# RG-LRU gate products one column tile later, the exponentials pinned behind the sigmoids, the delta rule's output split before the lz tiles, the rotary key's low part on GpSimd

## The chip, the cores and the metric

The kernel runs on one core of a Trainium2 chip. Its time is the device time of one execution in microseconds; where several runs are told, their median counts. The engines are named as the profile names them: PE (TensorE, matrix products; PEld is its loading of weights), DVE (VectorE), ACT (ScalarE), POOL (GpSimd) and SP (SyncE, which issues the DMA transfers).

## The reference

Two layers of an autoregressive trunk over 1024 tokens with 1024 features. Each layer normalises its input, projects it once to a wide row, hands slices of that row to three mixers, multiplies each mixer's output by a gate `silu(...)` from the same projection, and projects the 2048 gathered columns back, added to the input:

```
h = rmsnorm(x) ; proj = h @ w_in           # slices: q k v b a gz | mq mkv mkr mz | lx lz
A) o_a = rmsnorm(gated_delta_rule(...)) * silu(gz)             # 4 heads x 128
B) o_b = latent attention, 8 heads; the rotary key k_pe = rope(mkr) is shared by all heads; * silu(mz)
C) u = conv4(lx) + bias                                        # RG-LRU, 512 channels, 8 blocks of 64
   r = sigmoid(u @ w_r + b_r) ; i = sigmoid(u @ w_i + b_i)     # block-diagonal
   a = exp(-8 r softplus(-L)) ; b = sqrt(-expm1(2 log a)) * (i * u)
   h_t = a_t h_(t-1) + b_t ; o_c = h * silu(lz)
x = x + concat(o_a, o_b, o_c) @ w_out
```

The change touches mixer C, the way in which o_a comes to the output projection, and the rotary key of mixer B.

## The kernel before

**Layout and products.** Features lie on the 128 partitions, the 1024 tokens along the free axis; a half is 512 tokens (`H2`). Every operand of a product is kept as two tiles of type fp32r, a high and a low part (x = hi + lo). `mm3` issues three matmuls for each pair: ah·bh, ah·bl, al·bh (lines 121 to 123). `split` makes the two parts of an activation: a copy on ACT (line 127) and a subtraction on DVE or POOL (line 128). `load_w` does it for weights: a DMA into `wst`, the cast `whi` (on DVE for wide tiles, line 111; on ACT for narrow ones, line 109) and the subtraction `wlo` on POOL (line 112). `in_tile` makes one column tile of the input projection, 128 columns by 1024 tokens: 48 matmuls, 24 for each half, into a PSUM tile `pbig` of which there are two.

**The stage around the change.** After the delta rule of a layer, `lru` makes the four lx column tiles. For each column m it runs `conv` (one ACT step and three DVE steps, with raised priority), splits the result `u` by halves into `uh` and `ul` (the low part of the first half on POOL, of the second on DVE; one buffer each), loads the block-diagonal gate weights `w_lru[l, m]`, and makes the gate products: four groups of three matmuls into PSUM banks `pssc`, each followed by a sigmoid on ACT into `r` (tag lr) or `i` (tag li). Then u is multiplied by i, and tanh(8 r softplus) is taken into the tile of i (`th`). A second loop takes exp into the tile of r (now `a`), its square `a2` (tag lt, two buffers), and on DVE th = (a2 + 1) th, which is 1 - a² by way of the tanh. A third loop takes the square root, multiplies u by it and runs the scan (line 569). A fourth loop makes the four lz column tiles, the gate z (`silu2`: a tanh on ACT, a product on DVE; the tile z takes the slot of `uh` or `ul` in turn) and by halves `gate_split`: the product `of` on DVE (tag of, two buffers) and its split into `oh` and `ol` (POOL for columns 0 to 2, DVE for column 3). In `lru`'s text the delta rule's output comes last: four loads `oaf` from DRAM (tag li), each split into `oah` on ACT and `oal` on POOL.

**The output projection of this stage** (`out_proj`, called with `lru`'s result) goes over eight weight tiles of `w_o1`. Each has 48 matmuls, which read the four (oah, oal) pairs and the four (oh, ol) pairs by halves, into banks `pspr`; DVE adds a bank to the residual `xt` (line 92). There are three `xt` and two banks.

**The stage behind it** begins, still beside the output projection, with `split_latents`: five latents are loaded from DRAM and split, and the rotary key is turned (`rope`), copied twice into `kp` on ACT, and its low part `kl` is the difference, on DVE (line 663).

**What sets the order.** Each engine runs its instructions in an order that is fixed when the program is built. A scheduler picks them by priority: the place in the program's text, raised or lowered by `prio(±LOW)`, and by what is ready in its own model. `keep_in_program_order` pins one instruction behind the one traced before it on the same engine. So the text's order and the engines' order differ, and buffers (a tag with its number of slots) make a step wait until the reader of the slot's former content is done.

Of the kernel before, what the change touches and what calls it, by code (L numbers as in the profile page):

```python
# [9 lines left out]
F32 = mybir.dt.float32  # L10
F32R = mybir.dt.float32r
AF = mybir.ActivationFunctionType
ALU = mybir.AluOpType
AX = mybir.AxisListType

T = 1024
# [47 lines left out]
class Trunk:  # L64
# [18 lines left out]
        return self.ps.tile([128, H2], F32, name="ps" + tag, tag=tag)  # L83

    def act(self, out, in_, func, **kw):
        self.nc.scalar.activation(out, in_, func, **kw)  # L86

    def stt(self, out, in0, s, in1, op0, op1):
        self.nc.vector.scalar_tensor_tensor(out, in0, s, in1, op0, op1)  # L89
# [23 lines left out]
        return (hi[:, :n].rearrange("p (k c) -> p k c", k=nk),  # L113
                lo[:, :n].rearrange("p (k c) -> p k c", k=nk))

    def mm3(self, out, pairs):

        nc = self.nc
        n = len(pairs)
        for j, (ah, al, bh, bl) in enumerate(pairs):  # L120
            nc.tensor.matmul(out, ah, bh, start=(j == 0), stop=False)  # L121
            nc.tensor.matmul(out, ah, bl, start=False, stop=False)  # L122
            nc.tensor.matmul(out, al, bh, start=False, stop=(j == n - 1))  # L123

# [4 lines left out]


    def in_tile(self, l, *ms):

        if ms[0] not in self.ready:
            tiles = []
            for m in ms:
                hi, lo = self.early.pop(m, None) or self.load_w(self.i["w_in"][l, m], 8, 128)
                self.ready[m] = self.big()
                tiles.append((hi, lo, self.ready[m]))
            with self.prio(self.LOW):
                for n in range(2):  # L140
                    s = slice(n * H2, (n + 1) * H2)
                    for hi, lo, p in tiles:
                        self.mm3(p[:, s], [(hi[:, k], lo[:, k], self.hh[k][:, s], self.hl[k][:, s]) for k in range(8)])
        return self.ready.pop(ms[0])

    def conv(self, y, p, w, bias=None):

# [381 lines left out]
    def lru(self, l):  # L529
        nc, pa, par = self.nc, self.pa, self.par  # L530
        st, res = [], []
        for m in range(4):
            p = self.in_tile(l, MT_LX + m)
            u = pa.tile([128, T], F32, name="u", tag="lu", bufs=4)
            with self.prio(-self.LOW):
                self.conv(u, p, par[:, C_LCONV + 4 * m : C_LCONV + 4 * m + 4], bias=par[:, C_LCB + m : C_LCB + m + 1])
            uh = pa.tile([128, T], F32R, name="uh", tag="uh", bufs=1)
            ul = pa.tile([128, T], F32R, name="ul", tag="ul", bufs=1)
            for n, eng in ((0, nc.gpsimd), (1, nc.vector)):
                s = slice(n * H2, (n + 1) * H2)  # L540
                self.split(uh[:, s], ul[:, s], u[:, s], eng)
            hi, lo = self.load_w(self.i["w_lru"][l, m], 2, 128, pool=pa)
            gt = []
            for k in range(2):
                t = pa.tile([128, T], F32, name="lg", tag=("lr", "li")[k], bufs=4)
                cb = (C_LBR, C_LBI)[k] + m
                for n in range(2):
                    s = slice(n * H2, (n + 1) * H2)
                    pg = self.bank("sc")
                    self.mm3(pg, [(hi[:, k], lo[:, k], uh[:, s], ul[:, s])])  # L550
                    self.act(t[:, s], pg, AF.Sigmoid, bias=par[:, cb : cb + 1])
                gt.append(t)
            r, ii = gt
            self.tt(u, u, ii, ALU.mult)

            th = ii
            self.act(th, r, AF.Tanh, scale=self.c8[:, m : m + 1])
            st.append((u, r, th))
        for m in range(4):
            u, a, th = st[m]  # L560
            self.act(a, a, AF.Exp, scale=self.c8n[:, m : m + 1])
            a2 = pa.tile([128, T], F32, name="a2", tag="lt", bufs=2)
            self.act(a2, a, AF.Square)
            self.stt(th, a2, 1.0, th, ALU.add, ALU.mult)
        for m in range(4):
            u, a, th = st[m]
            self.act(th, th, AF.Sqrt)
            self.tt(u, u, th, ALU.mult)
            nc.vector.tensor_tensor_scan(th, a, u, 0.0, ALU.mult, ALU.add)
        for m in range(4):  # L570
            p = self.in_tile(l, MT_LZ + m)
            z = pa.tile([128, T], F32, name="lz", tag=("uh", "ul")[m % 2], bufs=1)
# [11 lines left out]
            res.append((oh, ol))  # L584
        for h in range(8 - self.MZ2, 8):
            self.gate_tile(l, MT_MZ + h, self.mzd[h], pa.tile([128, T], F32, name="z", tag="lt", bufs=2))
        oa = []
        for h in range(4):
            f = pa.tile([128, T], F32, name="oaf", tag="li", bufs=4)
            nc.sync.dma_start(f, self.oad[h])  # L590
            oh = pa.tile([128, T], F32R, name="oah", tag="lu", bufs=4)
            ol = pa.tile([128, T], F32R, name="oal", tag="lr", bufs=4)
            self.split(oh, ol, f, nc.gpsimd)
            oa.append((oh, ol))
        return oa + res


# [41 lines left out]
    def split_latents(self):  # L639
# [18 lines left out]
        for n in range(2):  # L658
            s = slice(n * H2, (n + 1) * H2)
            kr = self.rope(kx[0:64, s], 64, s)  # L660
            nc.scalar.copy(kp[0:64, s], kr)
            nc.scalar.copy(kp[64:128, s], kr)
            self.tt(kl[0:64, s], kr, kp[0:64, s].bitcast(F32), ALU.subtract)

            nc.scalar.copy(kl[64:128, s], kl[0:64, s].bitcast(F32))
        self.kp, self.kl = kp, kl
# [523 lines left out]
```

## Time and profile before

| | |
|---|---|
| Median of three runs | 2171.55 us (2168.96 to 2174.38) |
| The profiled execution, its own time | 2169.95 us |
| Its span | 2168.2 us |
| Mean granted clock of PE | 0.985 |
| ACT table loads | x81, 103.9 us |
| Low parts of weights on POOL (wlo) | x196, 316.2 us |

The span runs from the first to the last instruction of the profiled execution. Busy time counts the instructions that work on data; waiting in a queue is not in it. In rows of the timeline the first two numbers are the start (us from the span's start) and the duration, then engine, line, operation, output<-inputs and shape; a bracket at the end gives the idle time before the instruction on its engine and what ended it. Rows of grouped instructions have busy time and mean ns of one behind the first bar, and the idle time before them with its releaser behind the second. Rows of waits give engine, tile and line, what ended the wait, and then the idle time in us, the number of waits and the longest one. Rows of stretches give the stretch, its length, and the busy time of each engine with its number of instructions, the granted clock, the DMA share and GB/s. A row with x2 is two instructions that follow each other, drawn together.

### The profile page before, as it was taken

To read this page: it belongs to the slowest core of one execution; us is meant where nothing else is said; L and a number is where in the kernel's file an instruction comes from. 1 tells how busy PE (TensorE), PEld (TensorE's weight loads), DVE (VectorE), ACT (ScalarE), POOL (GpSimd) and SP (SyncE) were. 2 spreads that over 40 slices of the span, in tenths; PEclk is the share of its full clock that TensorE was granted. 3 is DMA by queue.
4 is the path that set the end of the run, shared out by engine and by line. 5 is a ranking of instruction groups with operands and counts; after the bars stand their busy time and mean duration, and the time that the engine had idled before them with its cause. 6 is when DMAs were issued, how large, how long until landed. Compare 5 with 4: busy or idle time off the path is not lost. (4 is left out here: it accounts for less than half of the span.)

```text
span 2168.2 us, 28796 instructions
## 1 busy us (share of the span) xinstructions
PE 2060.0 (95%) x10380; PEld 1685.0 (78%) x10380; DVE 1324.2 (61%) x2498; ACT 882.9 (41%) x1790; POOL 731.4 (34%) x784
## 2 busy tenths in 40 slices
PE   7999999999989999999899999999998999999997
PEld 4888877787768788878668888787876877878874
DVE  6647546555851777776675475474468337676766
ACT  6241344135720554444542413521376125444534
POOL 3222333234451333332241313333336323332322
PEclk9999999999999999999999999999999999999998
DMA  4223212323253116335421331134222520335172
GB/s 142 86 79 103 67 59 93 98 78 102 68 172 124 39 38 190 98 128 168 157 83 48 102 93 45 63 107 132 64 73 90 192 101 24 108 118 168 60 237 97
DMA packets 135103, 222.08 MB, mean 102 GB/s; under 512 B 37808, under 2 KB 60336, under 8 KB 134960
## 3 DMA queue, kind: packets, MB, share of 16 engines
q1 hardware_dynamic: 134960, 220.24, 31.3%
q8 instruction: 82, 1.34, 0.3%
q14 instruction: 61, 0.50, 0.1%
HBM read 147.31 MB, written 72.88 MB: 102 GB/s over the span
## 5 line engine op out<-in xcount | busy, mean ns | idle before, releaser
L112 POOL TENSOR_TENSOR wlo<-wst,whi 128x1024 fp32r<-128x1024 f32 (+3 forms) x196 | 316.2, 1614 | 831.0 <-DVE whi L111 302.0
L121 PE MATMUL pbig<-h,whi 128*128 128x512 f32 x1216 | 485.4, 400 | 9.2 <-ACT h L127 6.2
L123 PE MATMUL pbig<-h,wlo 128*128 128x512 f32 x1216 | 485.2, 399 | 4.0 <-POOL wlo L112 4.0
L122 PE MATMUL pbig<-h,whi 128*128 128x512 f32 x1216 | 484.5, 398 | 2.1 <-DVE h L128 1.0
L121 PEld LDWEIGHTS pbig<-h,whi 128*128 128x128 f32 x1216 | 231.4, 190 | 55.5 <-ACT h L127 7.0
L122 PEld LDWEIGHTS pbig<-h,whi 128*128 128x128 f32 x1216 | 230.7, 190 | 49.7 <-DVE h L128 3.5
L123 PEld LDWEIGHTS pbig<-h,wlo 128*128 128x128 f32 x1216 | 231.1, 190 | 48.8 <-POOL wlo L112 5.3
L86 ACT ACTIVATE P<-pS,mx,scq 128x512 f32<-128x512 f32 (+1 forms) x192 | 128.2, 671 | 154.0 <-DVE mx L89 82.5
L111 DVE CAST whi<-wst 128x1024 fp32r<-128x1024 f32 x92 | 78.5, 853 | 141.0 <-PE pbig L122 106.9
L95 POOL TENSOR_SCALAR P<-P,mx 128x128 f32<-128x128 f32 (+6 forms) x112 | 81.1, 725 | 211.3 <-DVE mx L778 128.6
L109 ACT CAST whi<-wst 128x256 fp32r<-128x256 f32 (+2 forms) x104 | 46.4, 446 | 203.8 <-DMA wst<-in_w_uk 100.0
L127 ACT CAST pth<-pstp 128x512 fp32r<-128x512 f32 x192 | 91.2, 479 | 75.4 <-PE pstp L807 75.4
L767 DVE TENSOR_REDUCE mx<-pS 128x1 f32<-128x512 f32 (+1 forms) x192 | 106.5, 555 | 16.6 <-PE pS L761 10.1
L128 DVE TENSOR_TENSOR ptl<-pstp,pth 128x512 fp32r<-128x512 f32 x192 | 104.8, 552 | 14.9 <-ACT pth L127 14.0
L86 ACT ACT_TABLE_LOAD x81 | 103.9, 1283 | 14.0 <-DVE kT L89 11.9
L807 PE MATMUL pstp<-con,P 128*128 128x128 f32 x576 | 98.1, 275 | 5.7 <-DVE P L782 5.0
L92 DVE TENSOR_TENSOR xt<-pspj,xt 128x512 f32<-128x512 f32 x96 | 66.2, 690 | 51.1 <-PE pspj L123 25.7
L807 PEld LDWEIGHTS pstp<-con,P 128*128 128x128 f32 x576 | 71.9, 141 | 25.8 <-DVE P L782 7.3
L121 PE MATMUL pspj<-lh,whi 128*128 128x512 f32 x208 | 84.0, 404 | 1.9 <-DVE q L128 1.8
L818 PE MATMUL pspo<-pth,vh 128*128 128x512 f32 x192 | 79.2, 413 | 2.9 <-ACT pth L127 2.9
L122 PE MATMUL pspj<-ll,whi 128*128 128x512 f32 x208 | 81.8, 393 | 0.0
L123 PE MATMUL pspj<-lh,wlo 128*128 128x512 f32 x208 | 81.5, 392 | 0.0
(270 smaller groups left out, 4574.8 us busy)
## 6 DMA issues: line engine op xcount, KB each, us to landing
wst<-in_w_in SPq DMA_DIRECT2D x76, 512.0 KB, 3.6
x<-xt SPq DMA_DIRECT2D x128, 256.0 KB, 3.4
xt<-x SPq DMA_DIRECT2D x112, 256.0 KB, 3.4
mzd<-z SPq DMA_DIRECT2D x16, 512.0 KB, 3.5
wst<-in_w_o SPq DMA_DIRECT2D x16, 512.0 KB, 3.5
mz<-mzd SPq DMA_DIRECT2D x32, 256.0 KB, 3.0
wst<-in_w_o SPq DMA_DIRECT2D x64, 128.0 KB, 2.1
xk<-x SPq DMA_DIRECT2D x32, 256.0 KB, 4.2
```

The lines of the kernel that those rows point to most:

```text
L86: self.nc.scalar.activation(out, in_, func, **kw)
L95: self.nc.gpsimd.tensor_scalar(out, a, s, 1.0, ALU.mult, ALU.mult)
L111: nc.vector.tensor_copy(hi[:, :n], st[:, :n])
L112: (eng or nc.gpsimd).tensor_tensor(lo[:, :n], st[:, :n], hi[:, :n].bitcast(F32), ALU.subtract)
L121: nc.tensor.matmul(out, ah, bh, start=(j == 0), stop=False)
L122: nc.tensor.matmul(out, ah, bl, start=False, stop=False)
L123: nc.tensor.matmul(out, al, bh, start=False, stop=(j == n - 1))
L127: self.nc.scalar.copy(hi, x)
L128: (eng or self.nc.vector).tensor_tensor(lo, x, hi.bitcast(F32), ALU.subtract)
L767: nc.vector.tensor_reduce(mx[:, j : j + 1], S[j], AX.X, ALU.max, negate=True)
L807: nc.tensor.transpose(tp[:, qi * 128 : qi * 128 + 128], P[qi][:, kb * 128 : kb * 128 + 128], self.ident)
L818: nc.tensor.matmul(po[:, w], vh[:, vs], th[:, w], start=(j == 0), stop=False)
```

## The change

Four edits, three of them in `lru`:

1. The gate products of a column stand behind the next column tile. A generator `gate_products` splits u and loads the gate weights, then pauses; the loop makes the next lx tile first and then lets the generator of the column before run on. Behind the fourth lx tile the first lz tile is made ahead (`in_tile_ahead`), and then the last gate products. The first matmul of each gate group of four is pinned behind the matmul traced before it (`behind`).
2. The first exp of the second loop is pinned behind the instruction traced before it on ACT, which is the tanh of column 3.
3. The delta rule's output is loaded and split before the lz tiles. Its loads take the two slots of tag lt, which hold the squares `a2`, in place of those of tag li.
4. The subtraction `kl` is issued on POOL.

```
-    def mm3(self, out, pairs):
+    def mm3(self, out, pairs, behind=False):
...
-            nc.tensor.matmul(out, ah, bh, start=(j == 0), stop=False)
+            first = nc.tensor.matmul(out, ah, bh, start=(j == 0), stop=False)
+            if behind and j == 0:
+                self.tc.keep_in_program_order(first)
...
+        def gate_products(m, u):
             uh = pa.tile([128, T], F32R, name="uh", tag="uh", bufs=1)
...
             hi, lo = self.load_w(self.i["w_lru"][l, m], 2, 128, pool=pa)
+            yield
...
-                    self.mm3(pg, [(hi[:, k], lo[:, k], uh[:, s], ul[:, s])])
+                    self.mm3(pg, [(hi[:, k], lo[:, k], uh[:, s], ul[:, s])], behind=(k == 0 and n == 0))
...
+        last = None
+        for m in range(4):
+            p = self.in_tile(l, MT_LX + m)
+            u = pa.tile([128, T], F32, name="u", tag="lu", bufs=4)
+            with self.prio(-self.LOW):
+                self.conv(u, p, ...)
+            for _ in last or ():
+                pass
+            last = gate_products(m, u)
+            next(last)
+        self.in_tile_ahead(l, MT_LZ)
+        for _ in last:
+            pass
         for m in range(4):
             u, a, th = st[m]
-            self.act(a, a, AF.Exp, scale=self.c8n[:, m : m + 1])
+            e = self.act(a, a, AF.Exp, scale=self.c8n[:, m : m + 1])
+            if m == 0:
+                self.tc.keep_in_program_order(e)
...
+        oa = []
+        for h in range(4):
+            f = pa.tile([128, T], F32, name="oaf", tag="lt", bufs=2)
...                      # the rest of this loop as it stood behind the lz tiles, where it had tag="li", bufs=4
         for m in range(4):
             p = self.in_tile(l, MT_LZ + m)
...
-            self.tt(kl[0:64, s], kr, kp[0:64, s].bitcast(F32), ALU.subtract)
+            nc.gpsimd.tensor_tensor(kl[0:64, s], kr, kp[0:64, s].bitcast(F32), ALU.subtract)
```

**ACT in layer 0, around the last gate products.** In these rows lg stands for the tiles of r, i, a and th, pssc is a gate product (so lg<-pssc is a sigmoid), lg with c8 the tanh, lg with c8n the exp, lz the tanh of a gate z. First before, from the sigmoids of column 2 to those of column 3's first gate:

```order
L86 ACT_TABLE_LOAD
L86 ACTIVATE lg_4227<-pssc_4228,par_185 128x512
L86 ACTIVATE lg_4227<-pssc_4233,par_185 128x512
L86 ACTIVATE lg_4227<-lg_4216,c8_488 128x1024
L86 ACT_TABLE_LOAD
L86 ACTIVATE lg_4216<-lg_4216,c8n_489 128x1024
L127 CAST uh_4300<-u_4295 128x512 x2
L86 ACTIVATE a2_4345<-lg_4216 128x1024
L86 ACT_TABLE_LOAD
L86 ACTIVATE lg_4312<-pssc_4313,par_185 128x512
L86 ACTIVATE lg_4312<-pssc_4318,par_185 128x512
```

and after, the rows that end with the square roots:

```order
L86 ACTIVATE lg_4378<-pssc_4384,par_185 128x512
L86 ACTIVATE lg_4378<-lg_4367,c8_488 128x1024
L86 ACT_TABLE_LOAD
L86 ACTIVATE lg_4084<-lg_4084,c8n_489 128x1024
L86 ACTIVATE lg_4367<-lg_4367,c8n_489 128x1024
L86 ACTIVATE a2_4392<-lg_4084 128x1024
L86 ACTIVATE a2_4396<-lg_4180 128x1024
L86 ACTIVATE lz_4511<-pbig_4462 128x1024
L86 ACTIVATE a2_4400<-lg_4276 128x1024
L86 ACT_TABLE_LOAD
L86 ACTIVATE lg_4095<-lg_4095 128x1024
L86 ACTIVATE a2_4404<-lg_4367 128x1024
L86 ACTIVATE lg_4191<-lg_4191 128x1024
```

Before, the exp of a column stands right behind its tanh and the tables change for each; after, the exps of columns 0 and 3 stand behind the last tanh, the squares of all columns behind them, and the square roots follow each other.

**POOL in layer 0, from the last gate split (ul<-u) to the end of the lz columns.** oal is the low part of the delta rule's output, ol that of a gated lz column (by halves), ll a latent's. First before:

```order
L128 TENSOR_TENSOR ol_4421<-of_4424,oh_4420 128x512
L112 TENSOR_TENSOR wlo_4571<-wst_4568,whi_4570 128x1024
L128 TENSOR_TENSOR ol_4421<-of_4428,oh_4420 128x512
L128 TENSOR_TENSOR oal_4641<-oaf_4638,oah_4640 128x1024
L128 TENSOR_TENSOR ol_4489<-of_4492,oh_4488 128x512
L128 TENSOR_TENSOR ol_4489<-of_4496,oh_4488 128x512
L128 TENSOR_TENSOR oal_4647<-oaf_4644,oah_4646 128x1024
L112 TENSOR_TENSOR wlo_4665<-wst_4662,whi_4664 128x1024
L128 TENSOR_TENSOR oal_4653<-oaf_4650,oah_4652 128x1024
L128 TENSOR_TENSOR oal_4659<-oaf_4656,oah_4658 128x1024
L128 TENSOR_TENSOR ol_4557<-of_4560,oh_4556 128x512
L128 TENSOR_TENSOR ol_4557<-of_4564,oh_4556 128x512
```

and after:

```order
L130 TENSOR_TENSOR oal_4422<-oaf_4419,oah_4421 128x1024
L112 TENSOR_TENSOR wlo_4665<-wst_4662,whi_4664 128x1024
L130 TENSOR_TENSOR oal_4428<-oaf_4425,oah_4427 128x1024
L130 TENSOR_TENSOR oal_4434<-oaf_4431,oah_4433 128x1024
L130 TENSOR_TENSOR ol_4445<-of_4448,oh_4444 128x512
L130 TENSOR_TENSOR oal_4440<-oaf_4437,oah_4439 128x1024
L130 TENSOR_TENSOR ol_4445<-of_4452,oh_4444 128x512
L130 TENSOR_TENSOR ol_4513<-of_4516,oh_4512 128x512
L112 TENSOR_TENSOR wlo_4729<-wst_4726,whi_4728 128x1024
L130 TENSOR_TENSOR ll_5206<-latf_5203,lh_5205 128x1024
L130 TENSOR_TENSOR ol_4513<-of_4520,oh_4512 128x512
L130 TENSOR_TENSOR ol_4581<-of_4584,oh_4580 128x512
```

All four oal subtractions now stand ahead of the second half of column 0's ol; before, they stood between those of columns 0 to 2. The last halves, of column 2, stand behind a weight tile's low part and a latent's.

**DVE in layer 0 at the rotary key.** xt is the residual sum that empties a bank of the output projection, rw the turned key, whi a weight cast. First before:

```order
L92 TENSOR_TENSOR xt_4761<-pspr_4763,xt_4761 128x512
L675 STREAM_SHUFFLE rw_5241<-kx_5237 64x512
L92 TENSOR_TENSOR rw_5241<-kx_5237,cos_5233 64x512
L92 TENSOR_TENSOR xt_4796<-pspr_4798,xt_4796 128x512
L92 TENSOR_TENSOR kl_5240<-rw_5241,kp_5239 64x512
L675 STREAM_SHUFFLE rw_5250<-kx_5237 64x512
L92 TENSOR_TENSOR rw_5250<-kx_5237,cos_5233 64x512
L92 TENSOR_TENSOR kl_5240<-rw_5250,kp_5239 64x512
L111 CAST whi_4920<-wst_4918 128x1024
L92 TENSOR_TENSOR xt_4825<-pspr_4827,xt_4825 128x512
L92 TENSOR_TENSOR xt_4860<-pspr_4862,xt_4860 128x512
```

and after:

```order
L92 TENSOR_TENSOR xt_4761<-pspr_4763,xt_4761 128x512
L92 TENSOR_TENSOR xt_4796<-pspr_4798,xt_4796 128x512
L697 STREAM_SHUFFLE rw_5241<-kx_5237 64x512
L92 TENSOR_TENSOR rw_5241<-kx_5237,cos_5233 64x512
L111 CAST whi_4920<-wst_4918 128x1024
L92 TENSOR_TENSOR xt_4825<-pspr_4827,xt_4825 128x512
L697 STREAM_SHUFFLE rw_5250<-kx_5237 64x512
L92 TENSOR_TENSOR rw_5250<-kx_5237,cos_5233 64x512
L92 TENSOR_TENSOR xt_4860<-pspr_4862,xt_4860 128x512
L111 CAST whi_4984<-wst_4982 128x1024
L92 TENSOR_TENSOR xt_4889<-pspr_4891,xt_4889 128x512
```

kl stood between two xt steps; after, DVE issues no kl, and the key's other steps are spread between xt steps and casts.

More of the change, by code (lines that the diff above doesn't have):

```diff
@@ L85, in act @@
     def act(self, out, in_, func, **kw):
-        self.nc.scalar.activation(out, in_, func, **kw)
+        return self.nc.scalar.activation(out, in_, func, **kw)
     def stt(self, out, in0, s, in1, op0, op1):
@@ L131, in in_tile, with in_tile_ahead @@
     def in_tile(self, l, *ms):
+        self.in_tile_ahead(l, *ms)
+        return self.ready.pop(ms[0])
+    def in_tile_ahead(self, l, *ms):
         if ms[0] not in self.ready:
@@ L143, in in_tile @@
                         self.mm3(p[:, s], [(hi[:, k], lo[:, k], self.hh[k][:, s], self.hl[k][:, s]) for k in range(8)])
-        return self.ready.pop(ms[0])
     def conv(self, y, p, w, bias=None):
@@ L531, in lru @@
         st, res = [], []
[L532 to L536, printed above, removed]
+        def gate_products(m, u):
             uh = pa.tile([128, T], F32R, name="uh", tag="uh", bufs=1)
@@ L558, in lru @@
             st.append((u, r, th))
+        last = None
[3 more added lines that the diff above has]
+            with self.prio(-self.LOW):
+                self.conv(u, p, par[:, C_LCONV + 4 * m : C_LCONV + 4 * m + 4], bias=par[:, C_LCB + m : C_LCB + m + 1])
+            for _ in last or ():
[5 more added lines that the diff above has]
+            pass
         for m in range(4):
             u, a, th = st[m]
-            self.act(a, a, AF.Exp, scale=self.c8n[:, m : m + 1])
+            e = self.act(a, a, AF.Exp, scale=self.c8n[:, m : m + 1])
+            if m == 0:
+                self.tc.keep_in_program_order(e)
             a2 = pa.tile([128, T], F32, name="a2", tag="lt", bufs=2)
@@ L569, in lru @@
             nc.vector.tensor_tensor_scan(th, a, u, 0.0, ALU.mult, ALU.add)
+        oa = []
+        for h in range(4):
+            f = pa.tile([128, T], F32, name="oaf", tag="lt", bufs=2)
+            nc.sync.dma_start(f, self.oad[h])
+            oh = pa.tile([128, T], F32R, name="oah", tag="lu", bufs=4)
+            ol = pa.tile([128, T], F32R, name="oal", tag="lr", bufs=4)
+            self.split(oh, ol, f, nc.gpsimd)
+            oa.append((oh, ol))
         for m in range(4):
@@ L586, in lru @@
             self.gate_tile(l, MT_MZ + h, self.mzd[h], pa.tile([128, T], F32, name="z", tag="lt", bufs=2))
[L587 to L594, printed above, removed]
         return oa + res
```

## The prediction

> **What bounds the kernel now.** I read the page's engine line first, then the PE clock and the busy time by stretches of the part that is changed, then PE's waits there, and last the timelines of PE, VectorE (DVE), GpSimd (POOL) and ScalarE (ACT).
>
> ```profile
> PE 2060.0 (95%) x10380; PEld 1685.0 (78%) x10380; DVE 1324.2 (61%) x2498; ACT 882.9 (41%) x1790; POOL 731.4 (34%) x784
> ...
> 503.30:596.60 93.30, 88.65 (x385) 71.54 (x384) 68.73 (x50) 66.87 (x75) 42.04 (x22) 1.00 0.24 75
> 596.60:615.20 18.60, 13.65 (x50) 9.98 (x49) 15.45 (x10) 6.64 (x10) 13.14 (x6) 0.91 0.48 166
> 642.00:652.00 10.00, 6.51 (x17) 4.83 (x16) 2.49 (x4) 1.85 (x3) 3.67 (x3) 0.66 0.36 115
> 1579.00:1665.50 86.50, 82.73 (x359) 66.54 (x358) 63.02 (x44) 65.64 (x74) 41.36 (x21) 1.00 0.22 71
> 1665.50:1686.80 21.30, 14.03 (x49) 10.14 (x48) 14.45 (x12) 7.28 (x10) 12.77 (x6) 0.84 0.48 169
> ```
>
> TensorE is the bound: only its stalls can be won or added. In each row the engines stand as PE, PEld, DVE, ACT, POOL, then the granted clock. Rows 1 and 4 are the lx and lz column tiles with the gate products, of layer 0 and layer 1. Rows 2 and 5 are the first weight tile of the output projection (48 matmuls). Row 3 is the stretch where the rotary key is turned, in layer 0. In rows 2 and 5 DVE and POOL are busy for most of the time while PE starves.
>
> ```profile
> 513.50 0.39 PE L121 MATMUL pbig<-h,whi 128*128 128x512 f32 x1
> 513.72 0.39 PE L122 MATMUL pbig<-h,whi 128*128 128x512 f32 x1
> ...
> 596.60 0.39 PE L121 MATMUL pspr<-oah,whi 128*128 128x512 f32 x1
> ...
> 608.59 0.63 PE L121 MATMUL pspr<-oah,whi 128*128 128x512 f32 x1
> 609.01 0.63 PE L122 MATMUL pspr<-oal,whi 128*128 128x512 f32 x1
> ...
> 615.16 0.39 PE L121 MATMUL pspr<-oah,whi 128*128 128x512 f32 x1
> ...
> 1665.52 0.39 PE L121 MATMUL pspr<-oah,whi 128*128 128x512 f32 x1
> ...
> 1686.82 0.39 PE L121 MATMUL pspr<-oah,whi 128*128 128x512 f32 x1
> ```
>
> From start to start a matmul takes 0.227 us (513.50 to 513.72 with the rounding), so a 48-matmul tile takes 10.9 us. The first weight tile runs from 596.60 to 615.16 (18.6 us) in layer 0 and from 1665.52 to 1686.82 (21.3 us) in layer 1. PE thus loses 7.7 and 10.4 us there. After a stall the step is 0.42 (608.59 to 609.01): half rate.
>
> **Gate products one tile later: a gain.** PE's waits in the tile stretch, first layer 0, then layer 1:
>
> ```profile
> PE pssc L122 <- POOL ul L128: 2.9, 3, 1.2
> PE pssc L121 <- ACT uh L127: 1.8, 1, 1.8
> ...
> PE pssc L122 <- POOL ul L128: 3.0, 3, 1.6
> PE pssc L121 <- ACT uh L127: 0.7, 1, 0.7
> ```
>
> The products wait for their own column's conv and split. In the new order a whole further tile (10.9 us) lies between a tile's end and its products, while eviction, conv and split take about 8 us (1.2 + 3.9 + 1.1 + 1.3 for ul). I count all 4.7 us of layer 0 and 3.7 us of layer 1 as won: 8.4 us. Bounds: 0, if a new late table load takes their place, and 8.4. I take the full value, because 5 us of slack remain when I follow ACT's new row order. The output projection could then begin at 596.6 - 4.7 = 591.9 and at 1665.5 - 3.7 = 1661.8.
>
> **Exps behind the sigmoids: off PE's path by itself, but it makes four scans late.** ACT's table loads go from 16 to 8 in this part of each layer by the order. Only the exps of columns 0 and 3 really move behind the last sigmoid; those of 1 and 2 stay between.
>
> ```profile
> L86 ACT ACT_TABLE_LOAD x16 | 20.5, 1283 | 0.3
> ...
> L86 ACT ACTIVATE lg<-pssc,par 128x512 f32<-128x512 f32 x16 | 10.4, 687 | 1.6 <-PE pssc L123 1.5
> L86 ACT ACTIVATE lg<-lg,c8n 128x1024 f32<-128x1024 f32 x4 | 4.6, 1153 | 0.0
> ...
> 541.99 2.28 DVE L569 TENSOR_TENSOR_SCAN lg<-lg,u 128x1024 f32<-128x1024 f32 x1
> ...
> 550.39 3.31 DVE L569 TENSOR_TENSOR_SCAN lg<-lg,u 128x1024 f32<-128x1024 f32 x1
> ...
> 567.89 2.29 DVE L569 TENSOR_TENSOR_SCAN lg<-lg,u 128x1024 f32<-128x1024 f32 x1
> ...
> 587.02 3.26 DVE L569 TENSOR_TENSOR_SCAN lg<-lg,u 128x1024 f32<-128x1024 f32 x1
> ```
>
> Eight loads of 1.28 us are 10.3 us of ACT per layer; ACT is 41% busy and I price that at nothing. Its cover is PE's tile work, and if ACT were the bound it would be worth up to 10.3 us per layer. The price is on DVE. Before, three scans are through by 570, under the tiles. After, by the row order of layer 0: three lz tiles follow the last gate products, so PE issues these at 591.9 - 3 x 10.9 - 2.7 = 556.5. Their last sigmoid is done at about 562.5; two DVE steps (1.2 each) lead to 564.3; tanh, load, two exps and a square (1.15 + 1.28 + 2.1 + 1.05) to 569.9. There the first a2 step of DVE begins, and all four columns hang behind it. Three more ACT steps, a load and a square root (5.5) give 575.4; u product, th step and the first scan (1.2 + 1.2 + 2.2) end at 580.0. All four scans, of which the trace had three done by then, are now to be run, and the gated outputs behind them.
>
> **The output's split ahead of the lz tiles: it queues ahead of what PE needs last.** In the new POOL order all four oal subtractions, two weight low parts and a latent stand ahead of ol of column 2. The loads do not come sooner: oaf now takes the slots of a2 (two), so its DMAs on SP wait for th steps 2 and 3 and then for oal of 0 and 1. POOL and DVE do not run side by side here:
>
> ```profile
> 503.34 0.69 DVE L111 CAST whi<-wst 128x1024 fp32r<-128x1024 f32 x1 [1.34 <-PE pbig L122]
> 566.63 1.22 DVE L92 TENSOR_TENSOR u<-u,lg 128x1024 f32<-128x1024 f32 x1 [1.22 <-ACT lg L86]
> 580.16 4.60 DVE L89 SCALAR_TENSOR_TENSOR of<-lg,lz 128x512 f32<-128x512 f32 x2
> 590.21 2.83 DVE L111 CAST whi<-wst 128x1024 fp32r<-128x1024 f32 x1
> ...
> 574.55 1.29 POOL L128 TENSOR_TENSOR ol<-of,oh 128x512 fp32r<-128x512 f32 x1 [10.23 <-ACT oh L127]
> 576.62 2.41 POOL L112 TENSOR_TENSOR wlo<-wst,whi 128x1024 fp32r<-128x1024 f32 x1 [0.78 <-DVE whi L111]
> 579.39 2.00 POOL L128 TENSOR_TENSOR ol<-of,oh 128x512 fp32r<-128x512 f32 x1 [0.36 <-ACT oh L127]
> 581.35 2.85 POOL L128 TENSOR_TENSOR oal<-oaf,oah 128x1024 fp32r<-128x1024 f32 x1
> 588.99 3.50 POOL L128 TENSOR_TENSOR oal<-oaf,oah 128x1024 fp32r<-128x1024 f32 x1 [0.85 <-ACT oah L127]
> 601.22 2.98 POOL L128 TENSOR_TENSOR ol<-of,oh 128x512 fp32r<-128x512 f32 x2
> ```
>
> The cast that takes 0.69 alone takes 2.83 at 590.21 and ends 0.6 after the POOL step that ran until 592.49. The two of steps (0.6 each alone) take 4.60 over two POOL steps. So each waits for the other's step: durations add. Alone, a 128x1024 step takes 2.4 and a 128x512 one 1.28 on POOL; DVE takes 1.15 and 0.6 a step, a scan 2.2. A check on the trace: from 576.62 to 604.20 POOL has 20.8 us of such steps (6 of 2.4, 5 of 1.28) and DVE 8.7 (two whole steps, a scan, seven halves or casts): 29.5 in 27.6 us, 0.93 of the sum.
>
> New order, layer 0: oal of 0 needs scan 0 (580.0) and a cast of 1.05, so it starts at 581.1. From there to ol of column 2's first half POOL has 7 x 2.4 + 5 x 1.28 = 23.2 us, and DVE two products, three scans, two weight casts and five of halves, 13.1 us. Sum 36.3, and 33.8 at 0.93. ACT adds a hop: a table load and lz2's tanh, which must wait for the last read of lz0, stand ahead of the cast for oal of 3; 2.5 us of it are uncovered. That is 617.4 to 619.9. Then come of, oh, ol of column 2's second half, of of column 3, a latent's subtraction and the last ol: 6.0 us, each behind the other. Fourteen matmuls remain (2.6 us after the last ol), and 1 us for half rate. The second weight tile starts at 627.0 to 629.5; I take 628.5, between them. Against 615.2 that is +13.3 us. Layer 1 has the same rows: 628.5 - 591.9 = 36.6 us from the first matmul, so 1661.8 + 36.6 = 1698.4 against 1686.8, +11.6 us. The 8.4 us won at the gates are in these two numbers already.
>
> By the Trainium skill (SBUF — State Buffer, Who interferes with whom) a DVE instruction with two SBUF inputs and a GpSimd one that reads SBUF exclude each other: the second fully blocks until the first finishes. By that rule alone the factor is 1 and the total below rises by 2 us, to 2191; the trace agrees on the blocking and differs by its 0.93. By the same skill's TensorE: Matmul & The Clock Gate (Part 1), an idle window of about 3.4 us halves the clock until PE was busy for as long; the long new stalls would then cost some 1.7 us more per layer than my 1 us, 2192 in all.
>
> **The rotary key's low part on POOL: a gain in layer 0 alone.**
>
> ```profile
> 644.07 0.68 DVE L92 TENSOR_TENSOR kl<-rw,kp 64x512 fp32r<-64x512 f32 x1 [3.17 <-ACT kp L661]
> ...
> 645.28 1.27 DVE L92 TENSOR_TENSOR xt<-pspr,xt 128x512 f32<-128x512 f32 x2
> ...
> 646.01 0.79 PE L121 MATMUL pspr<-oah,whi 128*128 128x512 f32 x1 [3.49 <-DVE xt L92]
> ```
>
> DVE sits 3.17 us at kl for ACT's cast, the evictions queue behind it, and PE has no bank: 17 matmuls in the 10 us of 642 to 652, where 44 fit, so 27 x 0.227 = 6.1 us are lost. On POOL kl holds up only the weight low parts, which have a pair of tiles (10.9 us) for 2.4 us of work; I count 6.1 us won. In layer 1 the same wait hides under filled banks: 0. Bounds 0 (POOL's own queue becomes late) to 6.1; the nearest row is the wait that goes.
>
> **Sum.** +13.3 + 11.6 - 6.1 = +18.8 us. The profiled execution took 2169.95 us, of which 2168.2 is its span; with the sum 2188.8. It stands 1.6 us under the median of the three runs, 2171.55, so I say 2189.
>
> **Rivals.**
> 1. POOL and DVE overlap in the new order (other steps meet than before). Then POOL's own 23.2 + 2.5 us from 581.1 lead to 607, the second weight tile starts at about 614 and 1661.8 + 22.1 = 1683.9: -1.2, -2.9 and -6.1, so 2160. Against it: every pair of rows above. It decides once 9.4 us of the 36.3 overlap in each layer, a quarter, where the check shows 7%.
> 2. The wait at the output projection ends when it ended before, because its last links (lz3's gate, of, ol of column 3) set it in both orders. Then the gate gain is only turned into this wait, and the key's 6.1 us are left: 2164. For it: before, too, column 3 ends the stall. Against it: of has two buffers, so column 2 and 3 queue behind ol of 0 and 1, now behind four oal.
> 3. The key's stall stays, through POOL's queue or a late kx load: 2195, with a longer half rate 2200. Against it: the tiles in between.
> 4. The exps do not go behind all sigmoids. That is what the order shows; it changes ACT alone and moves no time.
>
> **How the numbers follow.** My case 0.62, rival 1 0.12, rival 2 0.12, rival 3 0.14. My case's own range: the factor from 0.8 to 1.1 moves each layer by -5 to +6, so 2179 to 2200. The range for 8 in 10 reaches down into rival 2 and up to rival 3: 2164 to 2201. A measurement of this kernel can tell about 0.3%, 6.5 us, from no change. Rivals 1 and 2 are faster (0.24, of which I leave 0.02 to no change as rival 2 stands near that line), my case's low end gives 0.05 more to no change, the rest is slower.
>
> **What would show it.** Right: no PE wait at pssc for ul or uh; 8 table loads fewer per layer; the scans of layer 0 starting after 575 and DVE and POOL steps there at two to four times their own length; PE waiting on oal and ol for over 20 us in all before the second weight tile; no wait of PE for xt near the key. Wrong: short DVE steps beside running POOL ones, or the second weight tile at about 615 or earlier.

## The result

The changed kernel takes 2186.5 us (median of 4 runs, 2185.8 to 2190.5) against 2170.4 before (median of four, three of which are in the table above): 1.0081 times as long, 95% interval 1.0069 to 1.0093, or 16.1 us more. Forecast were 2189 and slower. Its profiled span is 2184.4 us, 16.2 more than before, so the profile carries the whole difference.

The page's engine line has hardly moved:

```profile
PE 2061.0 (94%) x10380; PEld 1683.1 (77%) x10380; DVE 1321.7 (61%) x2494; ACT 861.4 (39%) x1774; POOL 738.6 (34%) x788
```

The same stretches as before the change (engines in the order PE, PEld, DVE, ACT, POOL, then the granted clock): tiles and first weight tile of the output projection in layer 0, the rotary key's stretch, tiles and first weight tile in layer 1.

```profile
502.00:589.60 87.60, 87.60 (x385) 71.76 (x385) 52.73 (x42) 51.45 (x60) 31.74 (x16) 1.00 0.24 75
589.60:626.00 36.40, 18.45 (x49) 11.69 (x49) 27.92 (x19) 11.79 (x16) 24.84 (x12) 0.62 0.28 95
652.90:662.90 10.00, 10.00 (x46) 8.18 (x45) 5.05 (x6) 3.14 (x6) 8.46 (x7) 1.00 0.40 131
1582.40:1664.10 81.70, 81.70 (x360) 66.86 (x359) 47.54 (x36) 50.24 (x59) 28.74 (x15) 1.00 0.22 69
1664.10:1700.80 36.70, 18.44 (x49) 11.99 (x48) 27.87 (x19) 11.79 (x16) 24.80 (x12) 0.67 0.27 95
```

PE is busy for the whole of both tile stretches: no wait at a gate product is left, and they are 5.7 and 4.8 us shorter. What follows them is twice as long: 36.4 us for 48 matmuls against 18.6, 36.7 against 21.3. The key's stretch now holds 46 matmuls in 10 us, where it held 17. In that first weight tile PE waits, in layer 0, for:

```profile
PE pspr L124 <- POOL oal L130: 6.0, 3, 2.6
PE pspr L121 <- ACT oah L129: 5.9, 1, 5.9
PE pspr L124 <- POOL ol L130: 3.2, 1, 3.2
PE pspr L121 <- ACT oh L129: 2.7, 1, 2.7
```

These waits sum to 17.8 us; the rest of the 25.5 us above the 10.9 us of work is mostly half rate (granted clock 0.62). Behind the waits stand the late scans and the steps that DVE and POOL take in turn. The timeline of DVE, its scans:

```profile
576.43 2.28 DVE L591 TENSOR_TENSOR_SCAN lg<-lg,u 128x1024 f32<-128x1024 f32 x1
...
580.88 4.47 DVE L591 TENSOR_TENSOR_SCAN lg<-lg,u 128x1024 f32<-128x1024 f32 x1
...
594.09 4.43 DVE L591 TENSOR_TENSOR_SCAN lg<-lg,u 128x1024 f32<-128x1024 f32 x1
```

and of POOL, the split of the delta rule's output and the last ol:

```profile
579.95 3.27 POOL L130 TENSOR_TENSOR oal<-oaf,oah 128x1024 fp32r<-128x1024 f32 x1 [6.79 <-ACT oah L129]
...
590.29 6.09 POOL L130 TENSOR_TENSOR oal<-oaf,oah 128x1024 fp32r<-128x1024 f32 x2
...
603.54 2.36 POOL L130 TENSOR_TENSOR oal<-oaf,oah 128x1024 fp32r<-128x1024 f32 x1 [3.95 <-ACT oah L129]
...
618.08 1.60 POOL L130 TENSOR_TENSOR ol<-of,oh 128x512 fp32r<-128x512 f32 x1 [1.28 <-ACT oh L129]
```

The first scan ends at 578.7, and a scan beside a POOL step takes 4.4 us in place of 2.3. From there to POOL's last ol (619.7) it is 41.0 us. By their durations alone the steps that start in between sum to 42.3: on POOL 7 of 2.4 and 6 of 1.28 (24.5), on DVE three scans, four whole steps, and eleven casts or halves (17.8). In 1.8 of the 41.0 us (600.7 to 602.6) neither engine works: both wait for ACT, which loads a table there and then runs an lz tanh and a cast. In the other 39.2 us the 42.3 us of steps are done, a factor of 0.93.

### The profile page after: what moved, and what is told of

It reads as the page before. It is cut to its first block, busy times and chain, and to the rows that moved or that the text cites. A ratio compares the mean times of both kernels' runs of the same rounds, so it can differ in the third digit from the quotient of the medians.

```text
span 2184.4 us, 28792 instructions
## 1 busy us (share of the span) xinstructions
PE 2061.0 (94%) x10380; PEld 1683.1 (77%) x10380; DVE 1321.7 (61%) x2494; ACT 861.4 (39%) x1774; POOL 738.6 (34%) x788
## 5 line engine op out<-in xcount | busy, mean ns | idle before, releaser
L130 DVE TENSOR_TENSOR ptl<-pstp,pth 128x512 fp32r<-128x512 f32 x192 | 104.8, 552 | 14.3 <-ACT pth L129 13.3
L86 ACT ACT_TABLE_LOAD x65 | 83.4, 1283 | 24.5 <-DVE kT L89 11.9
```

The source lines that it names most:

```text
L86: return self.nc.scalar.activation(out, in_, func, **kw)
L130: (eng or self.nc.vector).tensor_tensor(lo, x, hi.bitcast(F32), ALU.subtract)
```

## The experiments

Twelve kernels; the median, the ratio to the kernel before (2171 us in the runs beside them), and the time from the start of the last lz matmul to the start of the second weight tile, which holds 10.9 us of work and PE's waits in the first weight tile of the output projection (where the mz tile is moved, from the last mz matmul):

| kernel | us | ratio, interval | layer 0 | layer 1 |
|---|---|---|---|---|
| before | 2171 | | 18.8 | 21.5 |
| changed (edits 1 to 4) | 2186.5 | 1.0081, 1.0069 to 1.0093 | 36.7 | 37.0 |
| without the exp pin (1, 3, 4) | 2161.9 | 0.9958, 0.9944 to 0.9972 | 16.8 | 16.8 |
| split late (1, 2, 4) | 2193.7 | 1.0101, 1.0086 to 1.0116 | 39.0 | 38.9 |
| only the exp pin (2) | 2197.9 | 1.0118, 1.0100 to 1.0136 | 35.6 | 36.1 |
| only the key (4) | 2169.7 | 0.9991, 0.9982 to 1.0000 | 16.8 | 21.9 |
| only gates later (1) | 2170.3 | 0.9992, 0.9981 to 1.0003 | 18.3 | 18.4 |
| only the split (3) | 2172.0 | 1.0007, 0.9995 to 1.0019 | 17.5 | 17.8 |
| changed, oal on DVE | 2174.2 | 1.0014, 1.0004 to 1.0024 | 28.5 | 29.1 |
| changed, tanh gates | 2185.0 | 1.0064, 1.0050 to 1.0078 | 34.2 | 35.5 |
| no pin, tanh gates | 2158.9 | 0.9946, 0.9932 to 0.9959 | 20.5 | 21.0 |
| the same, mz tile moved | 2194.2 | 1.0108, 1.0093 to 1.0124 | 11.1 | 11.1 |
| tanh gates, latent's cast behind | 2157.0 | 0.9933, 0.9921 to 0.9945 | 15.5 | 15.5 |
| the same, two halves | 2159.5 | 0.9951, 0.9938 to 0.9965 | 16.7 | 16.7 |

Every kernel with the pin on the exp has 28 to 39 us there, every one without it 11 to 22.

**Without the pin on the exp.**

```
             e = self.act(a, a, AF.Exp, scale=self.c8n[:, m : m + 1])
-            if m == 0:
-                self.tc.keep_in_program_order(e)
```

> The changed kernel without the pin on the first exp (edit 2 undone, edits 1, 3 and 4 kept). Built so, the exps, square roots and scans of columns 0 to 2 go back between the gate products, and the four oal subtractions go back between the ol ones on POOL, although the output's split still stands ahead of the lz tiles in the text. Theory A (the loss comes from the late scans, which the pin alone causes): the stall in the first weight tile of the output projection falls back to 8 to 10 us per layer, the gains at the gate products (4.7 and 3.7) and at the key (6.1) are left: 2170.4 - 14.5 = 2156. Rival B (the output's split ahead of the lz tiles costs the time wherever the exps stand): about 2186. Rival C (the gate gain only turns into a longer wait at the output projection, since its last links set the end): 2170.4 - 6.1 = 2164.

Measured 2161.9: 24.6 under the changed kernel and 9.1 (0.42%) under the one before, between A's 2156 and C's 2164 and nearer to C's number. C's mechanism is not what the trace shows, though: the stall at the output projection is shorter than before, not longer. B falls: the split is still ahead of the lz tiles in the text. Its stretch from the lz tiles to the second weight tile in layer 0:

```profile
594.10:610.92 16.82, 13.60 (x50) 10.17 (x49) 12.41 (x9) 5.43 (x9) 12.95 (x6) 0.90 0.42 144
```

PE's waits at the gate products of layer 0:

```profile
PE pssc L121 <- ACT lg L86: 2.9, 2, 2.4
```

and ACT around the fourth of them:

```profile
555.21 1.28 ACT L86 ACT_TABLE_LOAD   x1
556.50 1.16 ACT L86 ACTIVATE lg<-lg,c8n 128x1024 f32<-128x1024 f32 x1
557.69 1.06 ACT L86 ACTIVATE a<-lg 128x1024 f32<-128x1024 f32 x1
558.77 1.28 ACT L86 ACT_TABLE_LOAD   x1
560.06 1.26 ACT L86 ACTIVATE lg<-pssc,par 128x512 f32<-128x512 f32 x2
```

The stall is back at 16.8 us. But the gate gain is not whole: with exps between the sigmoids, PE waits for a bank that ACT empties only behind load, exp, square and load. So in layer 0 the pin is worth 4.7 us up to the end of the lz tiles (589.4 with it, 594.1 without, from the same start within 0.2) and costs 19.8 behind them.

**The split behind the lz tiles again.** The loop over `oaf` goes back to the end of `lru`, with its old tag:

```
-            f = pa.tile([128, T], F32, name="oaf", tag="lt", bufs=2)   # ahead of the lz loop
+            f = pa.tile([128, T], F32, name="oaf", tag="li", bufs=4)   # at the end
```

> The changed kernel with the delta rule's output split behind the lz tiles again, with tag li and four buffers (edit 3 undone; 1, 2 and 4 kept). Built so, POOL has all ol halves of columns 0 to 2 ahead of the last oal subtractions, and the scans stay late. Theory A (POOL's and DVE's steps from the first scan on add up, whatever their order): the same 23 us of POOL and 13 us of DVE lie between the first scan and the last part that the projection waits for, so 2180 to 2190. Rival B (the place of oal ahead of ol is what costs): most of the 17 us of loss goes, and with the gains of edits 1 and 4 it is 2156 to 2164.

Measured 2193.7, 7 over the changed kernel and 4 over the end of A's span. B falls: with all ol halves of columns 0 to 2 ahead of the last three oal, the stall is longer. In the trace 4.2 us of the 7 lie in the two stretches of the table; in layer 1's attention heads, which the edit does not touch, the run is 3.1 us longer.

**The pin alone**, the first experiment's lines added to the kernel before.

> The kernel before with the pin on the first exp alone (edit 2 alone). Built so, all four scans stand behind the last gate products, which here lie one tile later on PE against the changed kernel's, measured from the output projection: the last products run at 560 to 566, the output projection starts at 596.6. Theory A: the first scan ends some 7 us nearer to the output projection's start than in the changed kernel, so its stall is longer than there (36 us from the first matmul to the second weight tile): 38 to 43 us against 18.6 and 21.3 before, less what the table loads give back: 2170.4 + 35 to 45 = 2205 to 2215. Rival B (late scans cost only because the split stands ahead): within 2170 to 2176. Rival C (fewer table loads help): below 2168.

Measured 2197.9, +26 us: A's direction, but 7 under its lower end. The fourth gate products, which A took to stay in place, come 6.8 us earlier than before (the last at 559.0 against 565.8), with 12 table loads fewer in the program; that this makes up the 7 us is likely but not shown. The pin causes the loss without help from the other edits. The stretch in layer 0, and the first scan on DVE:

```profile
594.30:629.91 35.61, 16.48 (x50) 10.87 (x49) 27.61 (x17) 14.33 (x18) 25.51 (x12) 0.66 0.44 144
575.58 4.49 DVE L572 TENSOR_TENSOR_SCAN lg<-lg,u 128x1024 f32<-128x1024 f32 x1
```

In the kernel before, the first scan started at 541.99.

**The pin with cheaper gates.** The changed kernel with sigmoid(y) as (1 + tanh(y/2))/2:

```
-                    self.act(t[:, s], pg, AF.Sigmoid, bias=par[:, cb : cb + 1])
+                    self.act(t[:, s], pg, AF.Tanh, scale=0.5, bias=self.hb[:, cb : cb + 1])   # hb: half the bias
...
-            self.tt(u, u, ii, ALU.mult)
+            self.stt(u, ii, 1.0, u, ALU.add, ALU.mult)      # the output gate's factor 0.5 becomes 0.25
-            self.act(th, r, AF.Tanh, scale=self.c8[:, m : m + 1])                          # c8: 8 softplus
+            self.act(th, r, AF.Tanh, scale=self.c8[:, m : m + 1], bias=self.c8[:, m : m + 1])   # c8: 4 softplus
```

and the exp with scale and bias c8n (-4 softplus) in the same way.

> The changed kernel, pin and all, with the gates' sigmoids as tanh: no table load stands between tanh, exp and square, and POOL has the oal subtractions between the ol ones again (oal of 0, both halves of column 0, oal of 1 and 2, column 1, oal of 3, column 2). All four scans stay behind the last gate products. Theory A (late scans are the loss, the sum of POOL's and DVE's steps behind them stays): the scans start some 1 to 3 us earlier, 2186.5 - 4 = 2182, range 2178 to 2186. Rival B (the place of oal ahead of ol is the loss): 2160 to 2168.

Measured 2185.0, in A's range. This separates the two halves of the prediction's story: the first scan ends 3.5 us earlier than in the changed kernel (575.2) and ol stands between the oal steps, and still the stretch takes 34 us. Fewer table loads (57 in the program against 65) and another order on POOL together change little; the late scans are left. The stretch:

```profile
589.00:623.16 34.16, 18.37 (x51) 12.14 (x49) 28.63 (x19) 10.71 (x14) 24.67 (x10) 0.70 0.36 123
```

and POOL in it:

```profile
579.53 2.49 POOL L130 TENSOR_TENSOR oal<-oaf,oah 128x1024 fp32r<-128x1024 f32 x1 [7.77 <-ACT oah L129]
581.98 5.51 POOL L130 TENSOR_TENSOR ol<-of,oh 128x512 fp32r<-128x512 f32 x2
588.17 4.21 POOL L112 TENSOR_TENSOR wlo<-wst,whi 128x1024 fp32r<-128x1024 f32 x1 [0.69 <-issue]
592.34 7.61 POOL L130 TENSOR_TENSOR oal<-oaf,oah 128x1024 fp32r<-128x1024 f32 x2
```

**The split ahead alone** (edit 3 on the kernel before).

> The kernel before with the delta rule's output split ahead of the lz tiles in the text (edit 3 alone). Built so, the engines' order is that of the kernel before but for one exchange on POOL (an oal ahead of a half of ol) and one on ACT. Theory A (edit 3 by itself moves nothing, it only counts once the pin makes the scans late): 2170 to 2173. Rival B (the loads take the slots of the squares and come later, or the split queues ahead of ol): 2176 and more. Rival C (it is what gave the run without the pin its 9 us): 2164 to 2167.

Measured 2172.0, interval -0.05 to +0.19%: A. By itself the edit moves no time that can be told from zero. In the profiled execution the first weight tile of layer 1 is 3.7 us shorter than before, but the rest of that output projection is 5.5 us longer (81.4 against 75.9), with a wait of PE for xt of 3.5 us that before's layer 1 does not have.

**oal on DVE.**

```
-            self.split(oh, ol, f, nc.gpsimd)
+            self.split(oh, ol, f)
```

> The changed kernel with the four oal subtractions of a layer on DVE in place of POOL; all else kept. A 128x1024 step takes 2.4 us alone on POOL and 1.2 on DVE. Theory A (POOL's and DVE's steps exclude each other, so their durations add): the 36.3 us between the first scan and the last ol fall by 4 x 1.2 = 4.8, times 0.93, 4.5 us per layer: 2186.5 - 9 = 2177. Rival B (POOL's queue alone is the bound): POOL sheds 9.6 us per layer: 2167. Rival C (DVE alone is the bound): 4.8 us longer per layer: 2196.

Measured 2174.2, 12 us under the changed kernel: between A (2177) and B (2167), nearer to A, and not C. From the first scan's end (579.7) to POOL's last ol (614.4) it is 34.7 us, 6.3 less than the 41.0 of the changed kernel; the steps' own durations sum to 37.3, 5.0 less. The stretch:

```profile
590.40:618.91 28.51, 18.42 (x50) 11.43 (x48) 23.47 (x22) 12.75 (x17) 14.40 (x8) 0.76 0.36 128
```

and the second scan, which took 4.47 beside an oal and now runs alone:

```profile
581.89 2.28 DVE L591 TENSOR_TENSOR_SCAN lg<-lg,u 128x1024 f32<-128x1024 f32 x1
```

Work moved to the engine that the page shows busier (61 against 34% of the span), and the stall fell by 8 us a layer. Exclusion alone would give 4.5 us, POOL's queue alone 9.6. So the run rules out a bound by DVE alone, and by itself it does not part the other two. That the two engines block each other is seen in the rows: the scan takes 2.28 us alone and 4.47 beside an oal; and the sum of the steps against the time in which DVE or POOL works gives 0.93 again (34.5 us for 37.3). The profiled execution was the slowest of its twelve (2178.7): 8.7 us of what its two stalls win are lost in parts that the edit does not touch.

**The key alone** (edit 4 on the kernel before).

> The kernel before with the rotary key's low part on POOL alone (edit 4 alone). Theory: the wait of DVE at kl goes in layer 0 and PE loses no bank there: 2170.4 - 6.1 = 2164. Rival: the key's other DVE steps or POOL's queue put the wait elsewhere: 2170. Rival: both layers gain: 2158.

Measured 2169.7, -2.0 us (interval -3.9 to 0), under the 6 forecast. In the trace layer 0 gains 4.5 us over the key's stretch and layer 1 nothing. The wait shrank and moved. PE's wait for xt in layer 0's output projection, in the kernel before:

```profile
PE pspr L121 <- DVE xt L92: 3.5, 1, 3.5
```

and with edit 4:

```profile
PE pspr L121 <- DVE xt L92: 1.7, 1, 1.7
```

The timeline of DVE there, at its second shuffle:

```profile
639.93 0.01 DVE L675 LOAD_MASK_SELECT rw<-kx  x1 [3.97 <-POOL kl L663]
```

DVE no longer stands at kl, but the next half's `rw` takes a slot that POOL's kl must leave first. In the changed kernel an xt step and a cast stand ahead of that shuffle, and PE loses nothing. Why the timed gain is 2 and not the trace's 4.5 stays open: from the first product of layer 1's attention heads (bank pS) to the last (bank pspo), the profiled run takes 4.9 us more than before's, and every other kernel here takes 1.0 to 6.4 more, whichever way it moved, so that part of before's profile may have been a short one.

**Gates later alone** (edit 1 on the kernel before).

> The kernel before with the gate products one tile later alone (edit 1 alone). Built so, exps and square roots of columns 0 to 2 stand between the gates' sigmoids on ACT, as in the run without the pin. Theory A (edits add up): that run's -9.8 us less the key's -2.0 leaves -7 to -8: 2164. What its trace showed (new waits of 0.6 and 2.6 us of PE at the fourth products, for an ACT that is late by its table loads) should stand here too, in both layers. Rival B (the gain came only with edits 3 or 4): 2170 to 2172. Prediction's own term, the whole 8.4: 2163.

Measured 2170.3, -1.7 us (interval -4.1 to +0.7): B's number. The forecast new waits are there, in both layers, 3.0 us in layer 0 for the 4.7 removed. In layer 1 the first weight tile is 3.1 us shorter than before, but the rest of the output projection is 3.8 us longer (79.8 against 75.9), with a wait for xt of 1.9 us; in the run without the pin, which has edits 3 and 4 beside this one, it is 77.0. So the three edits do not add up (gates -1.7, split +1.5, key -2.0 alone, -9.1 together). PE's waits at the gate products of layer 0:

```profile
PE pssc L121 <- ACT lg L86: 3.0, 2, 2.5
```

**Tanh gates without the pin**, to take the table loads away and leave the scans early.

> The run without the pin, with the gates' sigmoids written as tanh: sigmoid(y) = (1 + tanh(y/2))/2, the factors put into the scales and biases of the exp, of tanh(8 r softplus) and of the output gate. Built so, exp, square and tanh need no change of table between them, and table loads are left at the square roots alone. Theory A (the waits of 0.6 and 2.6 us at the fourth gate products come from table loads): they go in both layers: 2161.9 - 6.4 = 2155.5. Rival B (the gain turns into a longer wait at the output projection, whose last links keep their time): 2160 to 2162.

Measured 2158.9, -12 us against before, but only 3 under the run with sigmoids, of the 6.4 forecast. PE's waits at the gate products of layer 0 fell from 2.9 to 1.6 us, and from the first gate product to the last lz matmul it is 2.6 us less in layer 0 (78.7 against 81.3) and 2.7 in layer 1. The first weight tile of the output projection is longer by more than that (20.5 against 16.8 us in layer 0), and its later part gives back 2.7 and 1.1. The trace shows why the first weight tile is longer. PE's longest wait there, in layer 0:

```profile
PE pspr L121 <- ACT oh L129: 3.9, 1, 3.9
```

and the timeline of ACT ahead of it:

```profile
597.96 1.05 ACT L129 CAST lh<-latf 128x1024 fp32r<-128x1024 f32 x1 [3.61 <-DMA latf<-latd]
598.91 0.59 ACT L86 ACTIVATE lz<-pbig 128x512 f32<-128x512 f32 x1
```

The first latent's cast waits 3.61 us for its DMA, and the tanh of lz column 3, whose tile was ready, is queued behind it.

**The latent's cast behind the last oh.** One line in `split`, used for the first latent:

```
+        c = self.nc.scalar.copy(hi, x)
+        if behind:
+            self.tc.keep_in_program_order(c)
```

> The run with tanh in place of the sigmoids, and the cast of the first latent (lh) pinned on ACT behind the last casts oh of lz column 3. In that run's trace ACT sits 3.6 to 3.8 us at this cast, for a DMA of the latent, with the tanh of lz column 3 queued behind it and PE waiting 4.1 to 4.3 us for that column's oh. Theory A (the latent's cast holds up the projection's last link): the tanh of column 3 runs some 4 us earlier, DVE and POOL share what is then gained, 3 to 4 us per layer are won: 2158.9 - 7 = 2152. Rival B (POOL and DVE set the end there too): 2157 to 2159.

Measured 2157.0, the fastest kernel here: 0.67% under before (0.55 to 0.79). Against the run without that line, -1.8 us, within the spread of the runs, and B's number; in the trace the stretch falls by 5.0 and 5.6 us, more than A's 3 to 4. Later in the output projection 1.9 us of that are lost again in layer 0 and 4.9 in layer 1, most of it a wait for xt (1.6 and 3.0). The stretch in layer 0:

```profile
591.20:606.62 15.42, 11.98 (x50) 9.01 (x49) 11.22 (x10) 4.96 (x7) 11.18 (x6) 1.00 0.44 155
```

and PE's wait that was 3.9:

```profile
PE pspr L121 <- ACT oh L129: 1.3, 1, 1.3
```

**Two halves.** In the first weight tile, both halves' first 21 matmuls ahead of the products of lz column 3:

```
+            for part in (range(7), range(7, 8)):
+                for n in range(2):
+                    for k in part:        # the three matmuls of pair k into the bank of half n
```

> As the run with the latent's cast behind, and in the first weight tile of the output projection the products of lz column 3 for both halves put behind the 2 x 21 others, so that PE has 4.8 us more of work while it waits for that column. Theory A: 2 to 4 us per layer less than without it, about 2147. Rival B (the second halves of columns 0 to 2 come no earlier from POOL than column 3, so the wait only moves): as without it.

Measured 2159.5, no better. The waits for column 3 are gone, but now both banks fill at the same time, and their eviction stands on DVE behind a latent's subtraction, which itself waits 3.4 us for ACT's cast of that latent:

```profile
PE pspr L121 <- DVE xt L92: 4.5, 1, 4.5
```

**An mz tile as cover.** `MZ2 = 1`: the last mz gate's tile comes between the lz tiles and the output projection.

> As the run with tanh in place of the sigmoids, and the last mz gate's column tile (48 matmuls, 10.9 us of PE) moved from beside the delta rule to between the lz tiles and the output projection, where PE waits 5 to 6 us per layer for DVE and POOL. Theory A (it fills that wait and is not missed where it was): 11 us less than without the move, about 2145. Rival B (it covered waits beside the delta rule, as PE is busy there by 7 to 9 tenths of a slice): PE loses up to 10.9 us per layer there, and the time is 2155 to 2167.

Measured 2194.2, 35 us over the run without the move and 27 over the end of B's range. The waits in the first weight tile are gone (11.1 us for 10.9 of work), but beside the delta rule PE now misses the tile. The longest wait there, in layer 0:

```profile
PE pbig L121 <- ACT sq L86: 9.6, 1, 9.6
```

At the last lz matmul of layer 0 the run is 6.1 us later than the run without the move (598.9 against 592.8), with the 10.9 us of the mz tile not yet done: 17 us are lost by then. The first weight tile wins back 9.3, but then PE waits 6.0 us for xt in the rest of the output projection, where the run without the move has no wait. What makes up the 17 us beyond the wait shown was not followed.

## Why the prediction was right, step by step

- **Gates, 4.7 and 3.7 us won.** The stage up to the output projection shrank by 5.7 and 4.8 us (all waits at pssc are gone). The step holds for this order alone: without the pin, exps, squares and table loads between the sigmoids make PE wait for a bank again (2.9 and 3.0 us). So "off PE's path by itself" was wrong, and the pin's order on ACT is what let the gate edit pay in full. The loads are part of it: with tanh gates and no pin 1.6 of the 2.9 us are left.
- **Late scans.** The first scan's end was put at 580.0; it was 578.7, in a trace whose stage began 1.3 us earlier.
- **Steps of DVE and POOL add.** Forecast from the first matmul to the second weight tile: 36.6 us in either layer; measured 36.4 and 36.7. From oal of 0 to ol of column 2's first half, forecast at 36.3 to 38.8 us with ACT's hop, it was 36.9 (579.95 to 616.80). The factor against the plain sum was 0.93 in the changed kernel, as in the prediction's check, once the 1.8 us are taken off in which both engines wait for ACT (the prediction priced that hop at 2.5), and 0.93 with oal on DVE. The Trainium skill (SBUF — State Buffer, Who interferes with whom) has the second step fully blocked, which alone would give 1; this case's traces agree on the blocking and stay 7% under the sum. The size of the step was right, and rival 1, which needed a quarter of overlap, was wrong.
- **The split "queues ahead of what PE needs last".** This part of the story failed, though not its number. With the split late the time was 7 us longer, with ol between the oal steps it was 1.5 shorter (and the scans 3.5 us earlier), and by itself edit 3 moved no time. So the split ahead is not what costs. Since all the work must be done behind the late scans, its order moves a few us; the pin moves 25.
- **Half rate, 1 us per layer.** About right on the path, though PE ran at half rate for far longer: it is busy 18.4 us in the stretch, for 10.9 us of work. The end of its last stall in layer 0 and the return to full rate, in the timeline of PE:

```profile
616.85 0.80 PE L124 MATMUL pspr<-ol,whi 128*128 128x512 f32 x1 [3.22 <-POOL ol L130]
617.45 0.63 PE L125 MATMUL pspr<-oh,wlo 128*128 128x512 f32 x1
...
622.40 0.39 PE L124 MATMUL pspr<-oal,whi 128*128 128x512 f32 x1
```

  Steps of 0.43 us last for 5.5 us after the stall; in the kernel before they lasted 3.5 (607.57 to 611.05). The Trainium skill (TensorE: Matmul & The Clock Gate, Part 1) gives a busy window of about 3.4 us, free-running and so not tied to the end of a stall; 5.5 is longer than one. But the product of column 3's first ol stood in the way in any case: DVE made that ol from 621.46 on (0.7 us), and PE took it at 622.86. At full rate PE would have come there earlier only to wait. By an estimate from these rows half rate cost some 0.7 us there, and the 1.7 us more that the Trainium skill's window would have added did not come.
- **The key, 6.1 us in layer 0, none in layer 1.** Measured in place: 6.5 and none. That kl on POOL won them is not shown. The edit alone won 4.5 us there in the trace and 2.0 in the time. And in the run with the pin alone, where kl is still on DVE and DVE still waits for ACT at it, the same part of the output projection is 6.1 us shorter than before and PE waits only 0.2 us for xt. There PE still has products to make while DVE stands at kl. Its row on DVE, the second kl of layer 0 in that run:

```profile
655.52 0.68 DVE L92 TENSOR_TENSOR kl<-rw,kp 64x512 fp32r<-64x512 f32 x1 [3.19 <-ACT kp L664]
```

  So the size was right, and a shift of the output projection against the key's steps is enough to bring it; the three runs in which layer 1 has a wait for xt that it did not have before (gates later alone, split alone, latent's cast behind) show the same from the other side.
- **Sum.** +12.2 and +10.5 us in the two stages against their own start, -6.5 at the key, +16.2 in all; forecast +13.3, +11.6, -6.1, +18.8. The rest, about zero, is scatter between the stages.
- **The signs.** No wait at pssc, 8 table loads fewer per layer, scans after 575, steps at twice their length and no wait for xt near the key: all came. "Over 20 us" of waits on oal and ol did not: PE's waits in the first weight tile sum to 17.8 us in layer 0, and 8.6 of them are put down to ACT's casts oah and oh.

Rival 2, that the gate gain turns into the wait at the output projection, has part of the truth once the pin is gone: with tanh gates the gain at the gates came back as a wait behind the latent's cast. Rival 4 was the order's own statement.

## What to carry to other kernels

Grouping activation functions saves table loads but makes every consumer of the group wait for its last member: before doing it, follow what hangs behind the group to the next stage's first product. Where two engines exclude each other, add their steps in a stretch and compare with the cover that PE gives; here order within the stretch was worth up to 7 us, and where it begins 25. Time won ahead of a later stall can come back there: three runs shortened the first weight tile of layer 1 by 3 to 6 us and lost as much in the rest of that output projection, behind the key's steps. When a wait is removed and the time stays, look for the instruction that stands idle at the head of the next queue: here a cast waiting for a DMA, with the critical tanh behind it.

## What the runs showed of the hardware that was not expected

DVE and POOL steps nearly add up over a whole mixed stretch: 0.93 of the sum in three stretches (27.6 of 29.5 us before, 39.2 of 42.3 after, 34.5 of 37.3 with oal on DVE), counting the time in which one of them works. So the sum of both counts, and giving work to the engine with the larger share of the span can win: 4.6 us more on DVE and 9.6 less on POOL shortened the stall by 8 us a layer. Tanh, exp and square follow each other on ACT with no table load between them; the timeline of ACT in the run with tanh gates and no pin (a is the square, lz a gate's tanh):

```profile
567.69 1.24 ACT L86 ACTIVATE lg<-lg,c 128x1024 f32<-128x1024 f32 x1 [2.26 <-DVE u L89]
...
569.35 1.24 ACT L86 ACTIVATE lg<-lg,c8n 128x1024 f32<-128x1024 f32 x1
...
571.00 1.06 ACT L86 ACTIVATE a<-lg 128x1024 f32<-128x1024 f32 x1
571.96 1.01 ACT L86 ACTIVATE lz<-pbig 128x1024 f32<-128x1024 f32 x1
572.99 1.28 ACT L86 ACT_TABLE_LOAD   x1
```

With the sigmoids written as tanh the loads of the whole program fell from 81 to 65 (1.28 us each), the number that the pin had reached, without late scans.
